# A two-layer mixture-of-experts trunk: expert overflow worked off pair by pair while the weights are in place

## The chip, the cores and the metric

The kernel runs on one NeuronCore of a Trainium2 chip, in one launch. The metric is device time in microseconds (us), the median of several executions. The engines are TensorE (PE, its weight loads shown as PEld), VectorE (DVE), ScalarE (ACT), GpSimd (POOL) and SyncE (SP, which issues nearly all weight transfers).

## What is computed

A trunk of two layers over 256 tokens of width 1024, in float32. Each layer mixes the tokens by four attention branches and then sends every token to 2 of 32 experts, each a gated feed-forward network of width 512:

```python
expert = (g_idx * EXPERTS_PER_GROUP + e_loc).reshape(-1)       # two experts for each token
...
def run_block(args):
    e, idx, g = args
    xb = xt[idx]
    hb = jax.nn.silu(xb @ w1[e]) * (xb @ w3[e])
    return (hb @ w2[e]) * g[:, None].astype(x.dtype)
...
y = jnp.zeros_like(xt).at[tok_buf].add(y_buf.reshape(-1, d))
```

The router chooses one of four groups and two of its eight experts, so an expert can get any number of tokens. With the reference's inputs the largest count is 27 in layer 0; in layer 1 one expert of 32, number 19, gets 33 tokens and no other more than 30. Only the numbers in the inputs decide that; the program is built without knowing them.

## The kernel before

**Pairs and places.** The 32 experts are taken two at a time: pair `i` (0 to 15) holds experts `2i` and `2i+1`. Each expert has `C = 32` places. A 0/1 matrix `Dm` (`placed`) puts tokens into places, `gather` (every fourth pair) collects the inputs of the next four pairs by matmul, `up_proj` multiplies by `w1` and `w3`, `glu` forms the gated hidden values, `down` multiplies by `w2`, and `combine` adds the results to the tokens' sums `acc`, which stay in PSUM for a whole layer.

**The weight ring.** A pair's weights are 8 MB of `up` and 4 MB of `w2`. They stream from HBM through `Ring`: 22 slots of 1 MB in the expert stage, made of eight tiles of two slots and six tiles of one. The list `jobs` gives the order of loads. `fill` goes through the list in order and stops at the first job that finds no room; a 2 MB job needs both slots of one tile, a 1 MB job takes a single slot first. `free` gives slots back and calls `fill`. This bookkeeping is done when the program is built; on the chip SP issues the loads in that order, and a load waits until the last reader of its slot is done. `up_parts` and `down_parts` say in how many jobs an expert's weights come. One further 1 MB tile (`early`) lies outside the ring and holds one part of pair 0.

**Order of the work.** PE's order is written out by hand (`manual_schedule`). The loop at L1437 lets the up-projection of pair `i` come before the down-projection of pair `i-1`; the loads are listed in that order too (`up(i)`, then `down(i-1)`). `up_proj` frees each part of the weights as soon as it has been used, `down` frees the rest. Pair 0's up-projection stands in `start_up` (L1190), ahead of the scatter matrix of pair 0 (L1193), which needs the gates `G` from `gates_of`.

**Overflow.** `overflow_list` counts how many further blocks of 32 places each expert needs and writes a list; it is advanced at pairs 4 to 6. At pair 7, `overflow` reads the count into every engine (L1213) and, if it is above zero, loops over the list (L1214): it loads that expert's weights once more by POOL's queue into ring slots held back for it (`over`, 5 MB from pair 5 to pair 7) and runs the block on its own.

Of the kernel before, what the change touches and what calls it, by code (L numbers as in the profile page):

```python
# [20 lines left out]
OVER = S * 2 // C  # L21
ALPHA = (2 * L) ** 0.25
# [24 lines left out]
def consts():  # L47
    p = np.arange(128)
    parts = {
        "ident": np.eye(128),  # L50
        "uinc": p[:, None] <= p[None, :],
        "ustr": p[:, None] < p[None, :],
        "causal": np.where(p[None, :] <= p[:, None], 0.0, NEG),
        "chunk": np.where(p[None, :] // 64 <= p[:, None] // 64, 0.0, NEG),
        "iota1": np.broadcast_to(np.arange(1, C + 1), (128, C)),
        "iota32": np.broadcast_to(np.arange(32), (128, 32)),
        "group": np.broadcast_to(np.arange(32) // 8, (128, 32)),
        "over": np.broadcast_to(C * np.arange(1, S // C), (128, S // C - 1)),
        "iota32c": p[:, None],
    }  # L60
# [54 lines left out]
def down_parts(e):  # L115

    return 2 if e < FINE - 2 else 1
# [84 lines left out]
def program(tc, I, out):  # L202
# [886 lines left out]
    def overflow_list(OH, pool, psp):  # L1089
# [8 lines left out]
        cnt = pool.tile([32, 2], F32, name="cnt")  # L1098
        V.tensor_copy(cnt[:, 0:1], T[:32, 0:1])
        V.tensor_scalar(act, K("over")[0:32], cnt[:, 0:1], None, op0=OP.is_lt)  # L1100
        V.tensor_reduce(cnt[:, 1:2], act, axis=AX.X, op=OP.add)
# [4 lines left out]
        lin = pool.tile([32, 2 * OVER + 1], F32, name="lin")  # L1106
# [9 lines left out]
        V.tensor_copy(lin[:, 2 * OVER:2 * OVER + 1], cnt[:, 1:2])  # L1116
        yield
        pl = psp.tile([128, 2 * OVER + 1], F32, name="T")
        nc.tensor.matmul(pl, ones[0:32], lin, start=True, stop=True)
        lst = pool.tile([128, 2 * OVER + 1], I32, name="lst")  # L1120
        V.tensor_copy(lst, pl)
# [5 lines left out]
    def experts(l, lg, logits, split, late, c2, acc, two_parts):  # L1127
# [4 lines left out]
        def start_up():  # L1132
# [51 lines left out]
            for tag, size in (("G", 64), ("neg", 2), ("ex", 32), ("gsm", 2), ("e2", 2), ("den", 1),  # L1184
                              ("hs", 512), ("Dg", 256)):
                p1.tile([128, size], F32, name="room", tag=tag)
# [24 lines left out]
        def overflow(lst, before):  # L1211

            n_over = nc.values_load(lst[0:1, 2 * OVER:2 * OVER + 1], min_val=0, max_val=OVER)  # L1213
            with tc.If(n_over > 0), tc.For_i(0, n_over, 1) as i:  # L1214
                ev = nc.values_load(lst[0:1, ds(i, 1)], engines=[mybir.EngineType.Pool, mybir.EngineType.DVE],
                                    min_val=0, max_val=NE - 1)
                W = [ring[(l, "over", j)] for j in range(2)]
                for j in range(2):
                    nc.gpsimd.dma_start(W[j], wup[l, ds(ev, 1)].rearrange("o p k s f -> (o p) (k s f)")[:, 4096 * j:4096 * j + 4096])
# [24 lines left out]
                for k in range(8):  # L1244
                    w = W[k // 4].rearrange("p (k s f) -> p k s f", k=4, s=2)
                    for s in range(2):
                        nc.tensor.matmul(ph[C * s:C * s + C], xo[:, k], w[:, k % 4, s], start=k == 0, stop=k == 7)
                nc.gpsimd.dma_start(W[0], wdown[l, ds(ev, 1)].rearrange("o p a j f -> (o p) (a j f)"))
# [10 lines left out]
                w = W[0].rearrange("p (a j d) -> p a j d", a=2, j=4)  # L1259
# [83 lines left out]
        def gated(i):  # L1343

            Dg = p1.tile([128, 2, 2, 2 * C], F32, name="Dg")
            c0 = 2 * C * (i % PQ)
            D4 = Dm[i // PQ].bitcast(F32)[:, :, c0:c0 + 2 * C].rearrange("p t (e s) -> p t e s", e=2)
            gv = G[:, :, 2 * i:2 * i + 2, None].to_broadcast([128, 2, 2, C])
            for a in range(2):
                nc.vector.tensor_tensor(Dg[:, :, a].rearrange("p t (e s) -> p t e s", e=2), D4, gv, op=OP.mult)  # L1350
            return Dg

        def scatter(i, Dg):

            pd = wkp.tile([128, 2, 128], F32, name="px" if i else "T")
# [6 lines left out]
            st[i] = dict(DT=DT, gate=gate)  # L1362

        def up_proj(i, bank="ph"):

            x = xg[i // PQ]
            c0 = 2 * C * (i % PQ)
            ph = wkp.tile([128, FE], F32, name=bank)
            part = 8 // up_parts(2 * i)
            for k in range(8):  # L1370
                keys = [(l, "up", 2 * i + e, k // part) for e in range(2)]
# [6 lines left out]
                if k % part == part - 1:  # L1378
# [9 lines left out]
        def glu(i, hs):  # L1388
# [10 lines left out]
            gTs[i] = gT  # L1399

        def down(i):
# [3 lines left out]
            keys = [[(l, "w2", 2 * i + e, a) for a in range(parts)] for e in range(2)]  # L1405
            py = wkp.tile([128, 512], F32, name="py")
            for j in range(4):
                for a in range(2):
                    for e in range(2):
                        w = ring[keys[e][a % parts]].rearrange("p (a j d) -> p a j d", a=2 // parts, j=4)  # L1410
                        o = C * (2 * a + e)
                        nc.tensor.matmul(py[o:o + C], gTs[i][:, j, e], w[:, 0 if parts == 2 else a, j],  # L1412
                                         start=j == 0, stop=j == 3)
            ring.free(*keys[0], *keys[1])
            gate = st[i]["gate"]
# [4 lines left out]
        def combine(i):  # L1420

            for t in range(2):
                for j in range(2):
                    for a in range(2):
                        r = slice(2 * C * a, 2 * C * a + 2 * C)
                        nc.tensor.matmul(acc[t][a], st[i]["DT"][r, t], out_parts[r, j], start=False,  # L1426
                                         stop=i == n - 1 and j == 1, skip_group_check=True)
                if i == n - 1:
# [7 lines left out]
        with tc.manual_schedule(engines={mybir.EngineType.PE}):  # L1436
            for i in range(n):  # L1437
                q, last = i // PQ + 1, i == n - 1
                if i:
                    hs = evacuated(up_proj(i))  # L1440
                    down(i - 1)
# [13 lines left out]
                if not last:  # L1455
                    scatter(i + 1, Dg)
                if i % PQ == PQ - 1 and not last:
                    for _ in gather(q):
                        pass
                if 4 <= i < 7:  # L1460
                    found = next(listing)
                if i == 7:
                    overflow(*found)
                    ring.free(*[(l, "over", j) for j in range(3)])
            down(n - 1)
            combine(n - 1)
# [34 lines left out]
def layout(inputs):  # L1501
# [18 lines left out]
    d["params"] = pack({"ident": C["ident"], "ln0": ln[0], **{n: C[n] for n in ("ustr", "iota1", "iota32", "group", "over", "iota32c")},  # L1520
# [34 lines left out]
```

## Time and profile before

| what | value |
|---|---|
| median of 3 runs | 1460.35 us (1459.32 to 1461.28) |
| the profiled execution | 1461.55 us, span 1459.9 us |
| mean granted TensorE clock | 0.899 of full speed |
| PE busy | 1162.8 us (80% of the span) |
| DVE, ACT, POOL busy | 524.3, 371.4, 89.0 us |
| moved by DMA | 494.89 MB, mean 339 GB/s |
| expert stage, layer 0 (first up-projection to last combine) | 276.37 to 705.60 us |
| expert stage, layer 1 | 978.21 to 1445.29 us |

The times are from one profiled execution; a group of instructions is written with its line, its engine, what it writes and reads, its count and its mean. In slices of the span a digit is a busy share in tenths. "Idle before" names what ended the wait.

### The profile page before, as it was taken

The numbers are of one execution on the slowest core, as the hardware profiler recorded it, in microseconds if no ns is written. First come the engines' busy times: TensorE is split into PE (matmuls) and PEld (weight loads), VectorE is DVE, ScalarE is ACT, GpSimd is POOL, SyncE is SP. The second block draws the span as 40 slices with busy tenths as digits, with TensorE's granted clock in tenths as the row PEclk, the third lists the DMA queues.
The fourth block names the chain that finished last, engine by engine and source line by source line (L and its number), as shares of the span: only waits on it lengthen the run. The fifth ranks groups of instructions, "written<-read, shape, count | busy, mean of one in ns | idle before, by whom it ended". The sixth has DMA issues, their size and how long they took to land.

```text
span 1459.9 us, 19103 instructions
## 1 busy us (share of the span) xinstructions
PE 1162.8 (80%) x7762; PEld 694.2 (48%) x7766; DVE 524.3 (36%) x1308; ACT 371.4 (25%) x792; POOL 89.0 (6%) x86
## 2 busy tenths in 40 slices
PE   8999999877776667766899999988766588667664
PEld 8999998523212112211699999962311152112111
DVE  6667786521011001100576777762101021001103
ACT  5556555311001000100365655531100010001000
POOL 2000030230000000000200003013000000000001
PEclk9999999999787988878999999999888779888986
DMA  9433677699999999999934339759999986999995
GB/s 385 177 116 130 245 312 291 275 425 428 429 427 426 427 428 426 428 428 418 410 120 174 123 145 383 287 218 426 426 427 427 427 331 251 426 428 429 425 424 229
DMA packets 47257, 494.89 MB, mean 339 GB/s; under 512 B 4928, under 2 KB 8512, under 8 KB 12864
## 3 DMA queue, kind: packets, MB, share of 16 engines
q1 hardware_dynamic: 46016, 486.23, 80.7%
q0 software_dynamic: 432, 6.29, 1.1%
q8 instruction: 62, 1.02, 0.3%
q10 hardware_dynamic: 720, 1.12, 0.2%
q14 instruction: 27, 0.22, 0.0%
HBM read 492.58 MB, written 1.05 MB: 338 GB/s over the span
## 4 chain that ended last, share of the span: by engine, by line
DMA 35%; PE 23%; DVE 4%; issue 4%; ACT 1%; SPq 1%; POOLq 0%; DVEq 0%; POOL 0%; ACTq 0%
DMA wslot<-in_up_dram 17%; DMA wslot<-in_down_dram 15%; PE ph L1376 5%; PE py L1412 4%; PE mm L503 3%; PE mm L505 3%; PE mm L504 2%; DMA wslot<-in_wmix_dram 1%; DMA ap<-in_attp_dram 1%; DVE split L474 1%; PE po L604 1%; SPq L259 1%; PE lg L505 1%; PE lg L503 1%; PE lg L504 1%
## 5 line engine op out<-in xcount | busy, mean ns | idle before, releaser
L1376 PE MATMUL ph<-wslot,xg 128*32 128x512 f32 x2048 | 315.8, 687 | 124.8 <-DMA wslot<-in_up_dram 119.5
L1412 PE MATMUL py<-wslot,gT 128*32 128x512 f32 x1024 | 190.6, 793 | 104.9 <-DMA wslot<-in_down_dram 104.8
L1418 DVE SCALAR_TENSOR_TENSOR ys<-py,gate,ys 128x512 fp32r<-128x512 f32 x32 | 24.0, 750 | 696.4 <-ACT ys L1417 696.4
L1376 PEld LDWEIGHTS ph<-wslot,xg 128*32 128x32 f32 x2048 | 76.4, 123 | 335.9 <-DMA wslot<-in_up_dram 174.0
L474 DVE TENSOR_TENSOR split<-wslot,split 128x512 fp32r<-128x512 f32 (+1 forms) x272 | 191.5, 716 | 96.2 <-ACT split L473 62.6
L473 ACT ACTIVATE split<-wslot 128x512 fp32r<-128x512 f32 (+2 forms) x276 | 168.8, 616 | 141.6 <-PE mm L505 121.8
L503 PE MATMUL mm<-hThi,split 128*128 128x256 f32 x704 | 202.5, 288 | 0.0
L505 PE MATMUL mm<-hThi,split 128*128 128x256 f32 x704 | 197.8, 281 | 0.5
L504 PE MATMUL mm<-hTlo,split 128*128 128x256 f32 x704 | 196.8, 279 | 0.0
L1412 PEld LDWEIGHTS py<-wslot,gT 128*32 128x32 f32 x1024 | 42.5, 138 | 243.6 <-DMA wslot<-in_down_dram 131.7
L1385 ACT ACTIVATE hs<-ph 128x512 f32<-128x512 f32 x32 | 19.1, 597 | 479.9 <-PE ph L1376 479.9
L503 PEld LDWEIGHTS mm<-hThi,split 128*128 128x128 f32 x704 | 132.5, 188 | 3.7 <-ACT split L473 1.3
L505 PEld LDWEIGHTS mm<-hThi,split 128*128 128x128 f32 x704 | 132.3, 188 | 2.6 <-DVE split L474 2.5
L504 PEld LDWEIGHTS mm<-hTlo,split 128*128 128x128 f32 x704 | 132.5, 188 | 0.5 <-issue 0.5
L1417 ACT ACTIVATE ys<-py,gate 128x512 fp32r<-128x512 f32 x32 | 22.0, 687 | 270.9 <-PE py L1412 270.9
L1426 PE MATMUL acc<-ys,DT 64*128 64x512 f32 x256 | 46.9, 443 | 19.5 <-ACT ys L1417 10.4
L1426 PEld LDWEIGHTS acc<-ys,DT 64*128 64x128 f32 x256 | 21.5, 184 | 39.9 <-ACT ys L1417 19.3
L574 ACT ACTIVATE P<-P,mx 128x128 f32<-128x128 f32 (+1 forms) x80 | 35.5, 445 | 14.2 <-DVE mx L572 14.2
L505 PE MATMUL lg<-oT,split 128*128 128x256 f32 x128 | 36.1, 282 | 1.4 <-DVE split L474 1.3
L503 PE MATMUL lg<-oT,split 128*128 128x256 f32 x128 | 36.0, 282 | 0.2
L504 PE MATMUL lg<-oT,split 128*128 128x256 f32 x128 | 35.8, 279 | 0.0
L828 ACT ACTIVATE gt<-mm,hbg 128x256 f32<-128x256 f32 x64 | 26.8, 470 | 25.0 <-PE mm L505 25.0
(341 smaller groups left out, 1422.9 us busy)
## 6 DMA issues: line engine op xcount, KB each, us to landing
wslot<-in_up_dram SPq DMA_DIRECT2D x96, 2048.0 KB, 27.6
wslot<-in_down_dram SPq DMA_DIRECT2D x52, 2048.0 KB, 28.9
wslot<-in_wmix_dram SPq DMA_DIRECT2D x32, 2048.0 KB, 8.7
wslot<-in_up_dram SPq DMA_DIRECT2D x64, 1024.0 KB, 10.7
wslot<-in_down_dram SPq DMA_DIRECT2D x24, 1024.0 KB, 15.3
wslot<-in_up_dram POOLq DMA_DIRECT2D x2, 2048.0 KB, 19.5
wslot<-in_wmix_dram SPq DMA_DIRECT2D x4, 832.0 KB, 13.6
wslot<-in_lnrows_dram SPq DMA_DIRECT2D x3, 1024.0 KB, 17.7
```

The source lines that it names most:

```text
L473: nc.scalar.activation(hi, w, AF.Copy)
L474: engine.tensor_tensor(lo, w, hi.bitcast(F32), op=OP.subtract)
L503: nc.tensor.matmul(ps, st[0], mv[0], start=start, stop=False)
L504: nc.tensor.matmul(ps, st[0], mv[1], start=False, stop=False)
L505: nc.tensor.matmul(ps, st[1], mv[0], start=False, stop=stop)
L574: nc.scalar.activation(dst, dst, AF.Exp, bias=mx[:, t, j:j + 1], scale=-1.0, accum_out=sm[:, t, j:j + 1])
L828: nc.scalar.activation(gt[:, j], pg[:, j], AF.Tanh, bias=hbg[:, cidx:cidx + 1], scale=0.5)
L1376: nc.tensor.matmul(ph[o:o + C], x[:, k, c0 + C * e:c0 + C * e + C], w[:, k % part, s], start=k == 0, stop=k == 7)
L1412: nc.tensor.matmul(py[o:o + C], gTs[i][:, j, e], w[:, 0 if parts == 2 else a, j], start=j == 0, stop=j == 3)
L1417: nc.scalar.activation(ys[:, 0], py, AF.Copy, scale=gate)
L1418: nc.vector.scalar_tensor_tensor(ys[:, 1], py, gate, ys[:, 0].bitcast(F32), op0=OP.mult, op1=OP.subtract)
L1426: nc.tensor.matmul(acc[t][a], st[i]["DT"][r, t], out_parts[r, j], start=False, stop=i == n - 1 and j == 1, skip_group_check=True)
```

## The change

- `overflow_list` now also gives, for each pair, the number of further blocks of its fuller expert. The old list keeps only the experts of the first and the last pair (`APART = (0, 15)`).
- The loop takes each pair to its end: up-projection, gated hidden values, down-projection, combine. Loads are listed in that order (`up(i)`, then `down(i)`), and `w2` comes as two 1 MB jobs for each expert except the last two.
- At the end of pairs 1 to 14 stands `again(i)`: every engine reads the pair's block count and branches; if it is above zero, a loop gathers the next 32 tokens of both experts and runs them with the weights that are in place. Only after it are the pair's 12 MB freed. Pairs 0 and 15 free their weights as they are used.
- The list is worked out within pair 0. One ring slot (`over`, 2) is held from pair 0 to the layer's end, 2 MB (`over`, 0) from pair 5 to pair 7; `overflow` for pairs 0 and 15 stays at pair 7 and reloads into that one tile.
- Pair 0's scatter matrix comes ahead of its up-projection.

The diff, cut to its core (left out: the constants, the arithmetic of the list, and arguments handed on):

```diff
 def down_parts(e):
-    return 2 if e < FINE - 2 else 1
+    return 1 if e >= NE - 2 else 2
...
-        for i in range(n + 1):
-            if i < n:
-                jobs += [job for both in zip(up(2 * i), up(2 * i + 1)) for job in both]
-            if i:
-                es = (2 * i - 2, 2 * i - 1)
-                jobs += down(es[0]) + down(es[1]) if i < n else last(es)
+        for i in range(n):
+            es = (2 * i, 2 * i + 1)
+            jobs += [job for both in zip(up(es[0]), up(es[1])) for job in both]
+            jobs += down(es[0]) + down(es[1]) if i < n - 1 else last(es)
+            if i == 0:
+                jobs += [((l, "over", 2), lambda t: None, 1)]
...
             if i == 5:
-                jobs += [((l, "over", 0), lambda t: None, 2), ((l, "over", 1), lambda t: None, 2),
-                         ((l, "over", 2), lambda t: None, 1)]
+                jobs += [((l, "over", 0), lambda t: None, 2)]
...
-            ph = up_proj(0)
             out_parts = flex.tile([128, 2, 512], F32R, name="ys", tag="A")
-            hs = evacuated(ph)
-            scatter(0, gated(0))
-            glu(0, hs)
             listing = overflow_list(OH, p1, wkp)
...
+        def again(i):
+            lst = found[0]
+            at = 2 * OVER + 1 + i
+            blocks = nc.values_load(lst[0:1, at:at + 1], min_val=0, max_val=S // C - 1)
+            with tc.If(blocks > 0), tc.For_i(0, blocks, 1) as b:
...
+                px = wkp.tile([128, 8, 2 * C], F32, name="py")
+                for k in range(8):
+                    for t in range(2):
+                        for i2, x in enumerate(two_parts):
+                            nc.tensor.matmul(px[:, k], x[:, t, k].bitcast(F32), Do[:, t], start=t == i2 == 0,
+                                             stop=t == i2 == 1)
+                affine_T(xo, px, 0)
+                DT, gate = scatter(gated(i, Do))
+                down(i, glu(evacuated(up_proj(i, xo, 0, False))), gate)
+                combine(DT, False)
...
-                if k % part == part - 1:
+                if free and k % part == part - 1:
                     ring.free(*keys)
...
-            ring.free(*keys[0], *keys[1])
...
+            found = None
+            DT, gate = scatter(gated(0, places(0)))
             for i in range(n):
-                q, last = i // PQ + 1, i == n - 1
-                if i:
-                    hs = evacuated(up_proj(i))
-                    down(i - 1)
+                q, last, apart = i // PQ + 1, i == n - 1, i in APART
+                hs = evacuated(up_proj(i, xg[i // PQ], 2 * C * (i % PQ), apart))
...
-                    Dg = gated(i + 1)
-                if i:
-                    glu(i, hs)
-                    combine(i - 1)
+                    coming = scatter(gated(i + 1, places(i + 1)))
+                if i == 0:
+                    next(listing)
+                if i % PQ == PQ - 1 and not last:
+                    for _ in gather(q):
+                        pass
+                gT = glu(hs)
+                if i == 0:
+                    next(listing)
...
+                down(i, gT, gate)
+                if apart:
+                    ring.free(*[key for keys in down_keys(i) for key in keys])
+                if i == 0:
                     found = next(listing)
+                combine(DT, last)
+                if not apart:
+                    again(i)
+                    ring.free(*[key for j in range(up_parts(2 * i)) for key in up_keys(i, j)])
+                    ring.free(*[key for keys in down_keys(i) for key in keys])
```

## Rows read from the trace of the kernel before

**Rows 1.** The page's slices of the span.

```profile
DMA  9433677699999999999934339759999986999995
```

**Rows 2.** Waits of PE, layer 0's expert stage: engine, line, releaser, total, times, longest.

```profile
PE ph L1376 <- DMA wslot<-in_up_dram: 57.6, 29, 3.9
PE py L1412 <- DMA wslot<-in_down_dram: 51.4, 16, 3.9
```

**Rows 3.** Windows: busy time of engines, granted clock, DMA share, GB/s.

```profile
400.00:500.00 100.00, 68.30 (x419) 21.76 (x416) 14.95 (x41) 7.92 (x15) 0.00 (x0) 0.86 1.01 427
269.00:270.00 1.00, 1.00 (x5) 1.00 (x6) 0.97 (x4) 0.00 (x0) 0.00 (x0) 0.50 0.11 41
278.00:279.00 1.00, 1.00 (x16) 0.29 (x12) 0.54 (x5) 0.39 (x3) 0.00 (x0) 1.00 0.00 0
280.00:281.00 1.00, 1.00 (x13) 0.26 (x8) 0.49 (x3) 0.65 (x4) 0.00 (x0) 1.00 0.92 377
```

**Rows 4.** Windows around the overflow of layer 1.

```profile
1190.00:1200.00 10.00, 10.00 (x43) 5.44 (x45) 2.16 (x9) 0.00 (x0) 0.48 (x1) 0.66 0.32 136
1200.00:1210.00 10.00, 5.53 (x21) 1.32 (x18) 0.57 (x2) 0.87 (x2) 0.04 (x1) 0.85 0.58 210
1210.00:1220.00 10.00, 9.63 (x22) 2.73 (x20) 1.36 (x2) 0.00 (x0) 0.00 (x0) 0.98 0.01 2
1220.00:1230.00 10.00, 9.91 (x80) 3.54 (x84) 0.00 (x0) 0.60 (x1) 0.00 (x0) 0.83 0.91 361
```

**Rows 5.** DMA queues: what POOL's own queue moved.

```profile
q0 software_dynamic: 432, 6.29, 1.1%
```

**Rows 6.** Timeline, start of layer 0's expert stage: start, duration, instruction.

```profile
276.37 7.07 PE L1376 MATMUL ph<-wslot,xg 128*32 128x512 f32 x64
278.32 0.80 SPq L282 DMA_DIRECT2D wslot<-in_up_dram  x2
282.34 0.49 DVE L1350 TENSOR_TENSOR Dg<-Dm,G 128x128 f32<-128x128 f32 x2
283.37 0.44 PE L1357 MATMUL T<-cp,Dg 128*128 128x128 f32 x2
```

**Rows 7.** Timeline, down-projections and a combine.

```profile
292.41 3.62 PE L1412 MATMUL py<-wslot,gT 128*32 128x512 f32 x32
...
297.67 0.95 PE L1426 MATMUL acc<-ys,DT 64*128 64x512 f32 x6 [0.28 <-DVE ys L1418]
...
336.37 5.33 PE L1412 MATMUL py<-wslot,gT 128*32 128x512 f32 x30 [3.80 <-DMA wslot<-in_down_dram]
```

**Rows 8.** The branch not taken in layer 0: its instructions, then the timeline.

```profile
L1213 PEldq TENSOR_LOAD <-lst x1: 492/492/492, 466.7 to 466.7; - x1
L1214 PEldq EVENT_SEMAPHORE  x1: 51/51/51, 467.9 to 467.9; - x1
467.58 0.28 PE L1316 MATMUL px<-Dm,lo 128*128 128x256 f32 x1
467.98 0.81 SPq L282 DMA_DIRECT2D wslot<-in_up_dram  x2
469.28 1.06 PE L1376 MATMUL ph<-wslot,xg 128*32 128x512 f32 x6 [1.42 <-ACTq L1214]
473.55 2.79 PE L1376 MATMUL ph<-wslot,xg 128*32 128x512 f32 x12 [3.21 <-issue]
```

**Rows 9.** The branch taken in layer 1: timeline.

```profile
1180.94 0.23 DVE L1222 TENSOR_SCALAR ope<-pos,before 128x2 f32 x1 [1.05 <-issue]
1193.87 0.61 PE L1240 MATMUL T<-cp,wslot 128*32 128x128 f32 x2
1207.57 5.00 PE L1264 MATMUL py<-wslot,wslot 128*32 128x512 f32 x8 [3.78 <-DMA wslot<-in_down_dram]
1220.09 8.77 PE L1376 MATMUL ph<-wslot,xg 128*32 128x512 f32 x64 [0.47 <-PE acc L1268]
1220.20 0.81 SPq L282 DMA_DIRECT2D wslot<-in_up_dram  x2
```

More of the change, by code (lines that the diff above doesn't have):

```diff
@@ L21 @@
 OVER = S * 2 // C
+APART = (0, NE // 2 - 1)
 ALPHA = (2 * L) ** 0.25
@@ L1097, in overflow_list @@
         act = pool.tile([32, nb], F32, name="act")
-        cnt = pool.tile([32, 2], F32, name="cnt")
+        cnt = pool.tile([32, 3], F32, name="cnt")
         V.tensor_copy(cnt[:, 0:1], T[:32, 0:1])
         V.tensor_scalar(act, K("over")[0:32], cnt[:, 0:1], None, op0=OP.is_lt)
-        V.tensor_reduce(cnt[:, 1:2], act, axis=AX.X, op=OP.add)
+        V.tensor_reduce(cnt[:, 2:3], act, axis=AX.X, op=OP.add)
+        V.tensor_scalar(act, act, K("apart")[0:32], None, op0=OP.mult)
+        V.tensor_scalar(cnt[:, 1:2], cnt[:, 2:3], K("apart")[0:32], None, op0=OP.mult)
         yield
@@ L1105, in overflow_list @@
         sel = pool.tile([32, 3, nb, OVER], F32, name="sel", tag="hs")
-        lin = pool.tile([32, 2 * OVER + 1], F32, name="lin")
+        n_l = 2 * OVER + 1
+        lin = pool.tile([32, n_l + 32], F32, name="lin", tag="ex")
         rk = pool.tile([32, nb], F32, name="rk")
@@ L1216, in overflow @@
                                     min_val=0, max_val=NE - 1)
-                W = [ring[(l, "over", j)] for j in range(2)]
-                for j in range(2):
-                    nc.gpsimd.dma_start(W[j], wup[l, ds(ev, 1)].rearrange("o p k s f -> (o p) (k s f)")[:, 4096 * j:4096 * j + 4096])
+                W = ring[(l, "over", 0)]
                 pe = p1.tile([128, 2], F32, name="ope")
@@ L1353, in scatter, with places @@
-        def scatter(i, Dg):
-            pd = wkp.tile([128, 2, 128], F32, name="px" if i else "T")
+                nc.vector.tensor_tensor(Dg[:, :, a].rearrange("p t (e s) -> p t e s", e=2),
+                                        D.rearrange("p t (e s) -> p t e s", e=2), gv, op=OP.mult)
+            return Dg
+        def places(i):
+            c0 = 2 * C * (i % PQ)
+            return Dm[i // PQ].bitcast(F32)[:, :, c0:c0 + 2 * C]
+        def again(i):
[3 more added lines that the diff above has]
+            with tc.If(blocks > 0), tc.For_i(0, blocks, 1) as b:
+                pe = p1.tile([128, 2, 2], F32, name="ope")
+                nc.vector.tensor_scalar(pe.rearrange("p t e -> p (t e)"), pos[:, :, 2 * i:2 * i + 2], K("over")[:, ds(b, 1)],
+                                        None, op0=OP.subtract)
+                Do = area(0, 2, 2 * C)
+                nc.vector.tensor_tensor(Do.rearrange("p t (e s) -> p t e s", e=2),
+                                        io[:, None, None, :].to_broadcast([128, 2, 2, C]),
+                                        pe[:, :, :, None].to_broadcast([128, 2, 2, C]), op=OP.is_equal)
+                xo = area(128, 8, 2 * C)
+                px = wkp.tile([128, 8, 2 * C], F32, name="py")
[8 more added lines that the diff above has]
+                combine(DT, False)
@@ L1356, in scatter @@
+        def scatter(Dg):
+            pd = wkp.tile([128, 2, 128], F32, name="px")
             for t in range(2):
@@ L1361, in scatter, with up_keys, down_keys, up_proj @@
             nc.vector.tensor_reduce(gate, pd.rearrange("p t s -> p (t s)"), axis=AX.X, op=OP.add)
[L1362 to L1368, printed above, removed]
+            return DT, gate
+        def up_keys(i, j):
+            return [(l, "up", 2 * i + e, j) for e in range(2)]
+        def down_keys(i):
+            return [[(l, "w2", 2 * i + e, a) for a in range(down_parts(2 * i))] for e in range(2)]
+        def up_proj(i, x, c0, free):
+            ph = wkp.tile([128, FE], F32, name="ph")
             part = 8 // up_parts(2 * i)
             for k in range(8):
-                keys = [(l, "up", 2 * i + e, k // part) for e in range(2)]
+                keys = up_keys(i, k // part)
                 for e in range(2):
@@ L1386, in evacuated, with glu @@
             return hs
-        def glu(i, hs):
+        def glu(hs):
             gT = p1.tile([128, 4, 2, C], F32, name="gT", bufs=2)
@@ L1398, in glu, with down @@
             nc.vector.scalar_tensor_tensor(gT.rearrange("p j e c -> p (j e) c"), th, 0.5, v[:, :, 1], op0=OP.mult, op1=OP.mult)
-            gTs[i] = gT
-        def down(i):
+            return gT
+        def down(i, gT, gate):
             parts = down_parts(2 * i)
-            keys = [[(l, "w2", 2 * i + e, a) for a in range(parts)] for e in range(2)]
+            keys = down_keys(i)
             py = wkp.tile([128, 512], F32, name="py")
@@ L1418, in down, with combine @@
             nc.vector.scalar_tensor_tensor(ys[:, 1], py, gate, ys[:, 0].bitcast(F32), op0=OP.mult, op1=OP.subtract)
-        def combine(i):
+        def combine(DT, last):
             for t in range(2):
@@ L1425, in combine @@
                         r = slice(2 * C * a, 2 * C * a + 2 * C)
-                        nc.tensor.matmul(acc[t][a], st[i]["DT"][r, t], out_parts[r, j], start=False,
-                                         stop=i == n - 1 and j == 1, skip_group_check=True)
-                if i == n - 1:
+                        nc.tensor.matmul(acc[t][a], DT[r, t], out_parts[r, j], start=False,
+                                         stop=last and j == 1, skip_group_check=True)
+                if last:
                     for a in range(2):
@@ L1454, in experts @@
                     next(residual)
[L1455 to L1460, printed above, removed]
-                    found = next(listing)
+                down(i, gT, gate)
+                if apart:
+                    ring.free(*[key for keys in down_keys(i) for key in keys])
+                if i == 0:
+                    found = next(listing)
+                combine(DT, last)
[3 more added lines that the diff above has]
+                    ring.free(*[key for keys in down_keys(i) for key in keys])
                 if i == 7:
                     overflow(*found)
-                    ring.free(*[(l, "over", j) for j in range(3)])
-            down(n - 1)
-            combine(n - 1)
+                    ring.free((l, "over", 0))
+                if not last:
+                    DT, gate = coming
+            ring.free((l, "over", 2))
             if l < L - 1:
```

33 lines of the change are left out of this document (18 added, 15 removed).

## The prediction

> **What bounds the kernel now.** I read the slices of the span first. The DMA engines are full, or nearly so, through both expert stages, except for one dip in layer 1 [rows 1]; before each stage they run out of work. PE's waits in layer 0's stage then name nothing but weights: 57.6 us for `up` and 51.4 us for `w2` [rows 2]. A window in the middle shows the same: 427 GB/s at a full DMA share, PE busy for 68 of 100 us [rows 3]. So the stage lasts as long as its transfers, plus any time in which no transfer runs. One ring slot (1.05 MB) takes 1.0486/427 = 2.46 us, a pair's twelve 29.5 us. A change counts here by the bytes that it saves and by the time in which the transfers stand still.
>
> They stand still twice. At the start of the stage the ring is full and nothing has been used: 41 GB/s at 269 us, none at 278, 377 again at 280 [rows 3], because the first slots come free only in the first up-projection, which begins at 276.37 [rows 6]. And in layer 1 the overflow stops SP in its loop: 136, 210, 2 and 361 GB/s in four windows of 10 us [rows 4]. Against 427 that lacks 2.9 + 2.2 + 4.3 + 0.7 = 10.0 MB, or 23.4 us. POOL's queue moved 6.29 MB more than a run without overflow needs [rows 5], or 14.7 us. Together the overflow costs 38.1 us. The two stages agree: by the times in the table above, that of layer 1 is 467.1 us long and that of layer 0 429.2, a difference of 37.9.
>
> **Part 1: the overflow's reload goes.** Expert 19 is in pair 9, which is worked off in place. The 38.1 us are gained, and what the new branch costs in pair 9 is set against them in part 4. Layer 0 has no overflow and gains nothing.
>
> **Part 2: the start.** Pair 0's scatter matrix now stands ahead of its up-projection in PE's hand-written order. Its input `Dg` is ready at 282.83 (282.34 + 0.49), and its transposes ran at 283.37 without waiting for PE's result [rows 6]. With them first, the up-projection begins at about 283.3 instead of 276.37, 6.9 us later, and nothing covers this, since the transfers already stand still. After such a wait PE is slow: an up-projection took 8.77 us after the overflow's half-clock stretch [rows 9] and 7.07 at full clock [rows 6]. I take 1.7 us more for the first freed slots. Start: 8.6 us in each layer (6.9 as the lower bound).
>
> **Part 3: slots come free later.** Today each part of `up` is freed as it is used. For pairs 1 to 14 all 12 slots now come free together, after combine and the branch. I followed the ring's own rule slot by slot (22 slots; a 2 MB job needs a whole tile) with durations from rows. From the landing of a pair's last weights: the down-projection takes 5.3 us (5.33 after a wait), ACT, DVE and combine another 2.6 (from 292.41 + 3.62 to 297.67 + 0.95) [rows 7].
>
> The branch: PE's register load starts at 466.7 and its closing semaphore at 467.9, while PE's last matmul ends at 467.86; SP issues at 467.98 [rows 8]. So the slots were released about 0.1 us after PE's work. Then PE ran six matmuls and stood 3.21 us with no releaser, having waited 1.42 before [rows 8]. Combine is a shorter cover than that gather, so I take 0.6 us for the release; the bounds are 0.1 and 4.6 (1.42 + 3.21, if the pause came first). The 4.6 us of PE are hidden wherever PE waits for weights afterwards. From SP's issue to flow is 1.4 us (278.32 to between 279 and 280.5) [rows 3, 6]. In sum 5.3 + 2.6 + 0.6 + 1.4 = 9.9 us pass before transfers for the next room flow.
>
> What covers these 9.9 us is what the ring can load ahead. By megabytes it would be 22 - 1 (held) - 12 = 9 slots, 22 us. But `w2` in 1 MB jobs breaks up two-slot tiles, and the list stops at the first job without room. The count gives four or six slots ahead in most pairs (9.8 or 14.7 us), so 9.9 us just fits, and only two (4.9 us) while `over` holds a tile. Pair by pair, the time without transfers:
>
> Pair 1: pair 0 frees 11 slots, 27.0 us of work. They run dry 3.5 (the first quarter of `up`, twice 1.77 at half clock) + 1.4 + 27.0 = 31.9 us after the first up-projection begins. Pair 0 then takes 8.8 (up) + 1.5 (evacuation and transposes) + 1.7 (`glu`) + 1.0 (the list, moved here; an estimate from its few short DVE steps) + 3.6 + 2.6 = 19.2, and pair 1 takes 7.1 + 1.5 + 1.7 + 3.6 + 2.6 + 0.6 = 17.1. With 1.4 to flow that is 37.7: 5.8 us lost. Pair 2 begins after the branch's pause and has eight slots' work ahead: 3.2. Pair 3, with a gather: 1.5. Pairs 5, 6 and 7, with `over` held: 5.0 + 3.3 + 2.1. The others: 0.6 together. In each layer 8.6 + 5.8 + 3.2 + 1.5 + 10.4 + 0.6 = 30.1 us.
>
> The same count with the order of before, the overflow left out, gives 703.2 us for the end of layer 0's stage, where the trace has 705.60.
>
> **Part 4: the branch taken.** Today's loop body runs from DVE's first step at 1180.94 to SP's next issue at 1220.20, 39.3 us, of which PE waited 3.8 for the reload [rows 9]; the way in adds some 1.5. That makes 37 us. The new body has both experts in it, but the up-projection's four column groups run side by side in either case, and combine is shorter. The bounds are 25 (today's PE work of about 33 us ran in good part at half clock, 0.66 granted in one window [rows 4]; at full clock some 12 go) and 49 (the gather, 12.3 us to 1193.87, doubles with its columns). No slot comes free meanwhile: 5.3 + 2.6 + 37 + 1.4 = 46.3 us against 9.8 of transfers ahead, a stop of 36.4 us. So the stop alone takes back nearly the whole gain, though no byte is loaded twice.
>
> **Edits at nothing.** The last pair's tail keeps its order, and the last weights arrive when they did. The list's extra steps are in pair 0. Register loads of ACT, DVE, POOL and SP run ahead of their next work. Behind each branch SP queues only loads that wait for that pair's slots anyway; without that cover they would cost what PE pays.
>
> **The sum.** On the profiled execution: 1461.55 - 38.1 + 2 x 30.1 + 36.4 = 1520. That execution lies 1.2 us above the median, so 1519.
>
> [...] The row shows PE going on for six matmuls behind a branch and pausing only then [rows 8]. [...]
>
> **The rivals.** *Every release waits for the code.* The new body is longer, so the target may lie farther off, and the 4.6 us may fall before PE's closing semaphore. Then 13.9 us pass instead of 9.9; pairs with four slots ahead no longer fit. The count gives 62.9 us for each layer and 30.6 for the taken branch: 1461.55 - 38.1 + 125.8 + 30.6 - 1.2 = 1579. For it: the pause exists. Against it: in the one row it came after.
>
> *The room counts by megabytes.* If nine slots are ahead after all (22.1 us), only the start and pair 1 cost (14.4 each layer), and the taken branch costs 46.3 - 22.1 = 24.2: 1475. Against it: the rule of the two-slot tiles.
>
> *The other side: only the start is paid.* If slots come free early enough that no later stop is left, the taken one included, 1461.55 - 38.1 + 17.2 - 1.2 = 1439. It is faster from the point where the stops of both layers sum to less than 38.1 us. For it: PE idles nearly a third of the stage. Against it: the room ahead is shorter than the loop body by any count.
>
> **How the numbers follow.** My count 0.50, with its own range 1500 to 1550 (release at 0.1 to 2 us, body at 25 to 49); every release late 0.28; room by megabytes 0.12; only the start 0.05; something between, near no change, 0.05. The range, 1488 to 1588, takes in the first two with the bounds. A difference of 0.2% is about what a measurement here can tell from none. Faster 0.06, same 0.03, slower 0.91; the time is that of my count, 1519.
>
> **What the new profile would show.** Right: the first `ph` matmuls in each layer some 7 us later behind PE's transposes; DMA windows below 427 GB/s at pairs 1, 2 and 5 to 7; one stop of 30 to 40 us in layer 1's middle; POOL's queue without its 6.29 MB. Every pair with a dip would mean the first rival; dips only at pair 1 and pair 9 the second. The forecast is wrong if the ring's room ahead is not what I counted, or if the release after the branch is far from 0.6 us.

## The result and the profile after

The changed kernel takes 1557.8 us (median of 4 runs, 1555.8 to 1559.3), against 1459.84 for the kernel before, run beside it: 1.067 times as long, interval 1.065 to 1.069. The forecast was 1519, with a range of 1488 to 1588. The profiled execution's span is 1556.4 us.

The slices of the page and one of its queues (the answers to [rows 1, 5]):

```profile
DMA  9333867689988989899934357659898889299996
...
q8 instruction: 103, 1.69, 0.4%
```

POOL's own queue, with its 6.29 MB [rows 5], is gone: the reload is away. But where nearly every slice of an expert stage had 9 tenths [rows 1], layer 0's stage now has five of 8, and layer 1's four of 8 and one of 2. The waits of PE show a new line (engine, line, releaser, total, times, longest):

```profile
PE ph L1412 <- DMA wslot<-in_up_dram: 165.9, 53, 9.9
PE ph L1412 <- PEq L1365: 61.0, 24, 6.5
...
PE px L1389 <- DVE Dg L1352: 13.1, 2, 6.5
```

L1365 is the `If` of the new branch: 24 times PE's next up-projection waited for PE's own sequencer. Windows of layer 0's middle and of the taken branch in layer 1 (columns as in [rows 3]):

```profile
400.00:500.00 100.00, 62.27 (x370) 20.62 (x368) 11.69 (x27) 7.16 (x13) 0.00 (x0) 0.83 0.94 390
...
1320.00:1330.00 10.00, 8.13 (x50) 2.36 (x46) 1.60 (x4) 0.98 (x2) 0.00 (x0) 0.78 0.99 419
1330.00:1340.00 10.00, 8.71 (x74) 6.26 (x66) 1.76 (x5) 0.69 (x1) 0.00 (x0) 1.00 0.27 112
1340.00:1350.00 10.00, 9.53 (x87) 4.20 (x85) 2.77 (x10) 0.16 (x1) 0.00 (x0) 1.00 0.00 0
1350.00:1360.00 10.00, 5.96 (x48) 2.21 (x52) 2.36 (x6) 1.51 (x3) 0.00 (x0) 1.00 0.01 2
```

390 GB/s stand where the kernel before has 427 [rows 3]. The taken branch stops the transfers for three windows, which lack 315 + 427 + 425 GB/s against 427, or 11.7 MB, or 27 us; some 2 us of these are what a pair loses anyway (below). PE runs the whole body at the granted clock 1.00.

The timeline of layer 0's start answers to [rows 6], and shows the scatter matrix first; the gather ahead of it ended some 3 us earlier than before, so that the up-projection begins 4.0 us later than in [rows 6], and some 7 us behind the gather instead of at once:

```profile
279.18 0.49 DVE L1352 TENSOR_TENSOR Dg<-Dm,G 128x128 f32<-128x128 f32 x2
...
279.82 0.66 PE L1389 MATMUL px<-cp,Dg 128*128 128x128 f32 x2 [6.55 <-DVE Dg L1352]
...
280.41 8.47 PE L1412 MATMUL ph<-wslot,xg 128*32 128x512 f32 x64
```

Two timelines at the ends of pairs 1 and 2 show the two kinds of release:

```profile
313.83 0.97 PE L1460 MATMUL acc<-ys,DT 64*128 64x512 f32 x6 [0.29 <-DVE ys L1452]
314.94 2.85 SPq L293 DMA_DIRECT2D wslot<-in_down_dram  x3
...
315.12 1.45 PE L1412 MATMUL ph<-wslot,xg 128*32 128x512 f32 x9 [0.32 <-PEq L1365]
...
331.70 0.96 PE L1460 MATMUL acc<-ys,DT 64*128 64x512 f32 x6 [0.29 <-DVEq L1365]
...
338.30 0.81 SPq L284 DMA_DIRECT2D wslot<-in_up_dram  x2
...
338.48 1.92 PE L1412 MATMUL ph<-wslot,xg 128*32 128x512 f32 x6 [5.82 <-PEq L1365]
```

After pair 1, SP issues 0.14 us behind combine (313.83 + 0.97 to 314.94). After pair 2 it issues 5.64 us behind it, and PE goes on only then. The line's own answer gives the branch instruction on PE, first in all, then in a window on each of these two (count, then least, median and longest duration in ns):

```profile
L1365 PEldq COMPARE_BRANCH  x31: 80/629/6616, 314.4 to 1512.3; - x31
...
L1365 PEldq COMPARE_BRANCH  x1: 371/371/371, 314.4 to 314.4; - x1
...
L1365 PEldq COMPARE_BRANCH  x1: 6032/6032/6032, 332.1 to 332.1; - x1
```

14 of the 28 pairs with a branch show one of 1.9 to 6.6 us, 67 us in sum; the others stay under 0.8. So both the forecast's count (release 0.6 us behind combine) and its first rival (every release late) describe about half of the pairs. For each pair I also worked out the transfers' loss: from one combine's end to the next, less the megabytes moved in between (the window's GB/s) at 427 GB/s. Before it is about 0 in nearly every pair; now it is 0.5 to 5.4 us in each of layer 0, 42 in sum.

### The profile page after: what moved, and what is told of

It is laid out like the page before. It is cut to its first block, busy times and chain, and to the rows that moved or that the text cites. A ratio compares the mean times of both kernels' runs of the same rounds, so it can differ in the third digit from the quotient of the medians.

```text
span 1556.4 us, 19679 instructions
## 1 busy us (share of the span) xinstructions
PE 1160.7 (75%) x7814; PEld 692.9 (45%) x7814; DVE 541.1 (35%) x1316; ACT 374.8 (24%) x793; POOL 87.5 (6%) x83
## 5 line engine op out<-in xcount | busy, mean ns | idle before, releaser
L1412 PE MATMUL ph<-wslot,xg 128*32 128x512 f32 x2048 | 356.7, 777 | 242.9 <-DMA wslot<-in_up_dram 165.9
L1412 PEld LDWEIGHTS ph<-wslot,xg 128*32 128x32 f32 x2048 | 83.9, 136 | 498.4 <-issue 275.1
L1448 PE MATMUL py<-wslot,gT 128*32 128x512 f32 x1056 | 149.8, 642 | 51.2 <-issue 29.8
L1392 DVE TENSOR_SCALAR DT<-px 128x256 fp32r<-128x256 f32 x33 | 14.0, 424 | 493.5 <-PE px L1389 493.5
L1352 DVE TENSOR_TENSOR Dg<-Dm,G 128x128 f32<-128x128 f32 x64 | 24.0, 413 | 84.6 <-PEq L1365 83.1
L506 PE MATMUL lg<-oT,split 128*128 128x256 f32 x128 | 36.1, 282 | 1.4 <-DVE split L475 1.3
L504 PE MATMUL lg<-oT,split 128*128 128x256 f32 x128 | 36.0, 281 | 0.2
```

The costliest lines, as they stand in the source:

```text
L504: nc.tensor.matmul(ps, st[0], mv[0], start=start, stop=False)
L506: nc.tensor.matmul(ps, st[1], mv[0], start=False, stop=stop)
L1412: nc.tensor.matmul(ph[o:o + C], x[:, k, c0 + C * e:c0 + C * e + C], w[:, k % part, s], start=k == 0, stop=k == 7)
L1448: nc.tensor.matmul(py[o:o + C], gT[:, j, e], w[:, 0 if parts == 2 else a, j], start=j == 0, stop=j == 3)
```

## The experiments

The theory from this profile was that freeing together and the pause in the branch both cost, with the start on top. The first four kernels ran on one chip. The interval is that of the ratio to the kernel before, which had 1460.94 us.

**The branch left out.**

```
-                    again(i)
```

> The changed kernel without its branch: the register load, the If and the loop behind combine are left out; slots of the 14 pairs still come free together behind combine. Leaves out the tokens past the 32 places in pairs 1 to 14 (here one token of expert 19 in layer 1). Theory (late release, part of it paid in the branch): PE's 24 long pauses in the branch go (61 us in sum, about half of it not covered by weights on their way), and the stop of about 24 us in pair 9 goes: 1557.8 - 24 - 2 x 16 = about 1502, and every pair's first slot comes free within 0.2 us of combine's end. Rival 1 (the pauses in the branch cost nothing because PE would wait for weights anyway): only the taken branch goes, 1557.8 - 24 = about 1534. Rival 2 (the branch is everything, freeing together costs nothing): about 1422 + 17 = 1440.

Measured: 1446.6 us (0.991, 0.989 to 0.992), 111 us less than the changed kernel; the theory had said 56. Not one pair loses more than 0.5 us of transfers apart from the last. The window 400 to 500 us of this kernel:

```profile
400.00:500.00 100.00, 66.20 (x395) 21.40 (x393) 11.40 (x28) 7.76 (x14) 0.00 (x0) 0.86 1.01 424
```

My reading of the edit was wrong in one point: SP doesn't issue behind combine here, but runs ahead. A load waits for the last instruction that read its slot. With the body gone this is the up-projection, whatever line frees the slot. So this run took away the late release too, and more had to be told apart.

**The branch with a body of one memset.**

```
-            with tc.If(blocks > 0), tc.For_i(0, blocks, 1) as b:
...
+            with tc.If(blocks > 0):
+                nc.vector.memset(area(0, 2, 2 * C), 0.0)
```

> The changed kernel with the branch in every pair, but its body is one small memset of VectorE instead of the whole second pass; nothing else of the pair's end moves. Leaves out what no_branch leaves out. Theory (the pause is code that has to be fetched because the target lies a long body behind the branch): PE's body is empty, the long pauses of 2 to 6.6 us vanish, the time is that of no_branch plus 14 x 2 x at most 0.5, between 1502 and 1510. Rival 1 (the register load and the compare cost it, or it's where other traffic delays any fetch): pauses stay in about half of the pairs and the time is that of no_branch plus about 32, some 1534. Rival 2: the branch costs nothing in either kernel, and both stand near 1534.

Measured: 1447.7 us (0.991, 0.989 to 0.993). A branch in 28 pairs costs about 1 us in all when its body is short and reads no slot. The branch instruction on PE:

```profile
L1365 PEldq COMPARE_BRANCH  x29: 70/202/325, 317.9 to 1404.4; - x29
```

**More room: `up` in 1 MB jobs.**

```
-    return 4 if e < FINE or e >= NE - 2 else 2
+    return 4
```

> The changed kernel with the up weights of all experts loaded in quarters of 1 MB (one slot each) instead of halves of 2 MB (a whole two-slot tile each); the branch and the frees stay. Theory (the stops come from the count of room: a 2 MB job waits for a whole tile, and what stands behind it in the list waits too): about nine slots ahead instead of four to six, so most stops of 2 to 5 us vanish; the count gives 27 and 32 us less for the two layers, about 1499. Rival 1 (the stops are the pauses of PE's branch themselves, whatever room there is): within 10 us of 1557.8. Rival 2 (smaller transfers run slower or cost SP more, as would show in full windows below 427 GB/s): slower than 1557.8.

Measured: 1501.5 us (1.027, 1.026 to 1.029), 56 us less; the count had said 59. The branch still pauses 6 us in half of the pairs, but with more slots ahead the transfers lose only 0.4 to 0.7 us in pairs 3 to 14 of layer 0. Its branch and its window:

```profile
L1365 PEldq COMPARE_BRANCH  x31: 70/447/6207, 314.3 to 1456.2; - x31
...
400.00:500.00 100.00, 63.19 (x378) 19.85 (x382) 11.88 (x28) 7.16 (x13) 0.00 (x0) 0.84 1.01 419
```

**The start undone.**

```
-            DT, gate = scatter(gated(0, places(0)))
             for i in range(n):
...
+                if i == 0:
+                    DT, gate = scatter(gated(0, places(0)))
```

> The changed kernel with pair 0's up-projection put back ahead of pair 0's scatter matrix in PE's order. Theory (the start is paid in full, nothing covers it): the first up-projection begins 6.5 us earlier in each layer and at full clock, so 2 x (6.9 + 1.7) = 17 us less, about 1541. Rival (pair 0 frees so much at once that a later stop, at pair 1 or 2, takes up what the start gains): between 1553 and 1558.

Measured: 1553.0 us (1.063, 1.058 to 1.068; four runs spread over 1543.8 to 1559.5): 5 us less and not 17; with this spread the 5 can hardly be told from none. The windows of this kernel and of the changed one say where the rest went. Up_first:

```profile
300.00:308.00 8.00, 6.21 (x54) 1.91 (x46) 1.60 (x4) 0.98 (x2) 0.00 (x0) 0.93 0.84 346
308.00:315.00 7.00, 5.58 (x40) 1.70 (x36) 1.41 (x3) 0.69 (x1) 0.56 (x1) 0.84 0.00 0
```

The changed kernel:

```profile
300.00:308.00 8.00, 6.81 (x62) 2.18 (x54) 1.08 (x3) 0.98 (x2) 0.00 (x0) 1.00 1.02 420
308.00:315.00 7.00, 5.11 (x40) 1.61 (x40) 1.31 (x4) 0.69 (x1) 0.00 (x0) 1.00 0.69 288
```

The first up-projection begins 5.6 us earlier (all but two of its matmuls, at 274.78 against 280.41), but pair 1's slots come free behind its branch at 314.3 instead of 314.9. What pair 0 freed earlier is used up earlier, and the transfers stand still until pair 1's end.

The next four, against 1459.72 us, tell the late release from the pause.

**Late release without a branch.**

```
-                    again(i)
+                    touch(i)
...
+            for n_key, key in enumerate(keys):
+                o = C * (n_key % 4)
+                nc.tensor.matmul(ph[o:o + C], ident[:, 0:C], ring[key][:, 0:512], start=True, stop=True)
```

> no_branch, with 12 short matmuls on PE behind combine that read one 512-column piece of each of the pair's 12 slots, so that the slots' last reader stands at the pair's end, as in the changed kernel, without any branch. Leaves out the second pass of pair 9. In no_branch the last reader of an up slot is the up-projection itself, so there the slots came free as used, whatever line frees them; that run took away the late release and the branch together, 111 us. Theory (both cost: late release by the count, and the pause on top): the count with a release 0.1 to 1.0 us behind combine gives 18 to 25 us more than no_branch for each layer, 1447 + 36 to 50 = 1483 to 1497. Rival 1 (late release costs nothing, all is the pause): 1447 to 1453. Rival 2 (all is late release, the pause is hidden): 1557.8 - 24 = about 1530.

Measured: 1514.2 us (1.038, 1.036 to 1.040), 68 more than no_branch and more than the theory's 36 to 50. SP issues 1.01 us behind combine here in nearly every pair. The 50 already took in a release that late, so the count of what late release costs is too low by some 18. In the next kernel the 12 matmuls stand in a body that is skipped and push no release back.

**Late release with a short branch.**

```
-            with tc.If(blocks > 0), tc.For_i(0, blocks, 1) as b:
...
+            with tc.If(blocks > 0):
+                nc.vector.memset(area(0, 2, 2 * C), 0.0)
+                touch(i)
```

> The changed kernel with the body of its branch cut to one memset and the same 12 short matmuls on the pair's slots, in every pair; never taken in pairs other than 9. Leaves out the second pass of pair 9. Theory (the pause comes from the length of the body): no PE pause above 0.5 us in the branch, SP's next load 0.1 to 0.3 us behind combine in every pair, and the time of held_no_branch plus at most 10. Rival (the branch itself, whatever its body, makes the wait): pauses of 2 to 6 us remain and the time is 40 us or more above held_no_branch.

Measured: 1499.4 us (1.027, 1.025 to 1.029). The branch never takes more than 0.33 us on PE, SP issues 0.13 us behind combine in nearly every pair, and yet the time is 52 us above the memset body. The only difference is that the body, hardly ever executed, has 12 matmuls that read the slots. For a release at 0.1 us the count had given 36.

```profile
L1365 PEldq COMPARE_BRANCH  x29: 70/207/332, 316.1 to 1460.1; - x29
...
400.00:500.00 100.00, 63.33 (x356) 19.45 (x356) 10.95 (x26) 7.15 (x13) 0.00 (x0) 0.80 0.92 384
```

In layer 0 the transfers lose 5.2 and 4.8 us in pairs 6 and 7, where `over` holds a tile, 1.3 to 3.3 in the other pairs up to 13, and 33 in sum. Pair 12 shows what the count had too small:

```profile
650.67 5.32 PE L1440 MATMUL py<-wslot,gT 128*32 128x512 f32 x26 [0.68 <-DMA wslot<-in_down_dram]
...
658.63 0.81 SPq L284 DMA_DIRECT2D wslot<-in_up_dram  x2
...
658.00:659.00 1.00, 0.69 (x8) 0.24 (x6) 0.00 (x0) 0.00 (x0) 0.00 (x0) 1.00 0.24 98
659.00:660.00 1.00, 0.86 (x4) 0.00 (x0) 0.00 (x0) 0.00 (x0) 0.00 (x0) 1.00 1.01 229
660.00:661.00 1.00, 0.56 (x8) 0.26 (x12) 0.00 (x0) 0.00 (x0) 0.00 (x0) 1.00 0.44 164
```

SP issues 8.0 us after the last weights let the down-projection go on, as counted (5.3 + 2.6 + 0.1), and four slots, 9.8 us of transfers, were still to come. But the rate has fallen before SP issues and is full again only 2.4 us after it. The three windows lack 0.8 MB, 1.9 us, where the count, with full rate to the last byte and 1.4 us from issue to flow, had next to nothing.

**The long body, but without the slots.**

```
+                other = two_parts[0][:, 0].bitcast(F32).rearrange("p k q -> p (k q)")[:, 0:512]
...
-                down(i, glu(evacuated(up_proj(i, xo, 0, False))), gate)
+                down(i, glu(evacuated(up_proj(i, xo, 0, False, other))), gate, other)
...
+                                         w[:, k % part, s] if other is None else other,
...
```

> The changed kernel with the whole body, instruction for instruction, but its matmuls on weights read a piece of the activations instead of the ring's slots, so that the body doesn't hold them. Its second pass works on wrong weights. Theory (the pause matters only because the release waits for it): PE's pauses of 2 to 6.6 us in the branch stay in about half of the pairs, yet transfers run at 425 GB/s through the pairs, and the time is 1447 plus 0 to 15 for the branch taken in pair 9. Rival (the pause costs PE time that the stage needs): 1447 + 40 to 60 = about 1500.

Measured: 1482.0 us (1.016, 1.014 to 1.017). The pauses are all there (14 of 5.9 to 6.8 us), and the transfers run on:

```profile
L1365 PEldq COMPARE_BRANCH  x31: 70/702/6772, 315.5 to 1435.5; - x31
...
L1365 SPq EVENT_SEMAPHORE  x11: 27/28/20797, 1235.9 to 1285.0; - x11
...
400.00:500.00 100.00, 64.49 (x386) 21.19 (x382) 11.40 (x26) 7.15 (x13) 0.00 (x0) 0.84 1.01 423
```

In pair 9 they lose 23.6 us, nearly as much as in the changed kernel, though this body holds no slot: SP itself waits in the loop, 20.8 us on one semaphore. The rest, 1482.0 - 23.6 - 1447.7 = 11 us, is left for the pauses when no release waits for them. My bound of 1462 was too low: I had allowed at most 15 us for the taken branch.

**The second pass ahead of the main one.** The whole computation is done.

```
+                if not apart:
+                    again(i)
-                hs = evacuated(up_proj(i, xg[i // PQ], 2 * C * (i % PQ), apart))
+                hs = evacuated(up_proj(i, xg[i // PQ], 2 * C * (i % PQ), True))
...
-                if not apart:
-                    again(i)
-                    ring.free(*[key for j in range(up_parts(2 * i)) for key in up_keys(i, j)])
-                    ring.free(*[key for keys in down_keys(i) for key in keys])
```

> The changed kernel with the branch of pairs 1 to 14 put ahead of the pair's own up-projection instead of behind its combine; the slots are freed as the main pass uses them, and the two scatter matrices are two fixed tiles. The whole computation is done. Theory (the branch costs when it is the last reader of the slots): the main pass is the last reader again; the pauses stay but lie where PE waits for weights, and the body of pair 9 runs while that pair's weights and the next ones still land, so 1447 plus 0 to 10, faster than before. Rival 1 (the pauses shift every up-projection and so every release): about 1447 + 40 to 60 = 1500. Rival 2 (the taken branch stops the transfers by its 24 us here too): about 1471.

Measured: 1481.0 us (1.016, 1.014 to 1.017): 77 us less than the changed kernel, yet not the theory's 1447 to 1457. The taken branch now costs the transfers only 7 us. But pairs 1 and 2 of layer 0 lose 2.3 and 8.9 us, and pair 2 of layer 1 loses 6.4. There, I take it, the ring is still full from its start, so PE is what the transfers wait for, and a pause of 6 us ahead of an up-projection delays its frees. The next kernel tries that. Of the 33 us above small_body these losses make 25; the others are not placed.

**That, without a branch in pairs 0 to 2, and the start undone.**

```
-APART = (0, NE // 2 - 1)
+APART = (0, 1, 2, NE // 2 - 1)
...
```

The rest of the edit is that of again_ahead and that of up_first.

> again_ahead, and pair 0's up-projection again ahead of its scatter matrix, and pairs 1 and 2 listed with 0 and 15 for the loop that reloads, so that no branch stands in the pairs in which the ring still works off its full start. The whole computation is done. In again_ahead the transfers still lost 2.3 and 8.9 us in pairs 1 and 2 of layer 0, 6.4 in pair 2 of layer 1, and some 12 us at each start. Theory (these losses go, the taken branch keeps its 7): 1481 - 17 - 2 x 7 to 9 = 1446 to 1450, faster than the kernel before. Rival (the start's gain is taken up by a later stop, as in up_first): 1460 to 1464, no change against before.

Measured: 1449.8 us (0.9925, 0.991 to 0.994, five runs, against 1460.55): 0.7% faster than the kernel before, and within the theory's range. With the reference's inputs no expert of pairs 0 to 2 overflows; where one does, it is loaded again. The windows around the taken branch of this kernel:

```profile
1220.00:1230.00 10.00, 9.59 (x84) 8.12 (x88) 2.61 (x11) 0.00 (x0) 0.00 (x0) 1.00 1.01 428
1230.00:1240.00 10.00, 6.16 (x44) 1.50 (x40) 1.18 (x5) 0.00 (x0) 0.00 (x0) 0.88 1.01 425
1240.00:1250.00 10.00, 7.05 (x54) 1.90 (x46) 0.94 (x3) 1.67 (x3) 0.00 (x0) 0.95 0.82 350
1250.00:1260.00 10.00, 8.40 (x73) 2.98 (x73) 1.14 (x3) 0.00 (x0) 0.00 (x0) 1.00 0.67 238
```

The body runs while weights land, and what is left of the stop of 27 us is 77 + 189 GB/s in two windows, 6 us.

**The old overflow's price, and the start's without a late release.** The first leaves out `overflow(*found)` in the kernel before, the second makes the edit of up_first in no_branch.

> The kernel before without the call of its overflow loop: no register load, no If, no reload. Leaves out the tokens past the 32 places. Theory (the prediction's part 1: reload 14.7 us and stop 23.4 us in layer 1): 1461.55 - 38.1 - 1.2 = about 1422. Rival (only the megabytes count, the stop is made up by the ring's room): about 1445.

> no_branch with pair 0's up-projection put back ahead of its scatter matrix. Leaves out the second pass of pair 9. In up_first, with the branch, this edit gave 5 us instead of 17, and the transfers stood still 6.9 us at pair 1 instead: there pair 1's slots came free only behind its branch. Theory (without a late release nothing takes the gain up): 1446.6 - 2 x (6.9 + 1.7) = about 1429. Rival (the start is worth only what up_first showed): 1440 to 1444.

Measured: 1422.45 us (0.973, 0.972 to 0.975), as forecast, so the old overflow costs 1460.55 - 1422.45 = 38.1 us; and 1431.6 us (0.980, 0.978 to 0.982), so the start costs 1446.6 - 1431.6 = 15.0, near the 17.2 that were forecast.

**`w2` in whole jobs.**

```
-    return 1 if e >= NE - 2 else 2
+    return 2 if e < FINE - 2 else 1
```

> The changed kernel with the w2 weights of most experts loaded in one job of 2 MB again instead of two of 1 MB; the branch, the frees and the bytes stay. Theory (room is counted by the ring's rule, tile by tile: with 2 MB jobs alone only whole tiles serve, and odd single slots stay empty): the count puts 90 us of standing transfers into a layer where it puts 34 for the changed kernel, so 1557.8 + 2 x 56 = about 1670. Rival 1 (megabytes decide): within 10 us of 1557.8. Rival 2 (larger jobs fit better and help): under 1540.

Measured: 1683.5 us (1.152, 1.150 to 1.154, against 1461.06), 126 us more than the changed kernel where the count had said 112. Its branch and its window:

```profile
L1365 PEldq COMPARE_BRANCH  x31: 80/446/4267, 316.5 to 1651.0; - x31
...
400.00:500.00 100.00, 56.70 (x290) 15.85 (x282) 9.21 (x22) 5.01 (x9) 0.00 (x0) 0.72 0.85 356
```

The same bytes in larger jobs make it much slower; by the count, because they find no whole tile.

## Why the prediction was right in part, step by step

The medians give a ladder, from the kernel before to the changed one:

- Part 1, the old overflow: -38.1 us, forecast and measured.
- Part 2, the start: +15.0, forecast 17.2. Behind the late release it is worth some 5 at most (up_first), because pair 1's end then decides; the forecast added both in full.
- The remaining edits (no_branch_up_first less before_no_overflow): +9.1, forecast 0. The traces place about half of it: with one slot held from pair 0, a slot less has landed when each stage begins (below, up to 270 us, the first the kernel before without its overflow; layer 1 has the same difference), which is 2.46 us in each layer. The rest is spread over the stages (426 GB/s in the middle of layer 0's against 427) and not settled.

```profile
q1 hardware_dynamic: 8672, 64.40, 61.4%
q1 hardware_dynamic: 8528, 63.36, 60.3%
```

- A branch with a short body (small_body less no_branch): +1.1, forecast 0.
- Part 3, slots freed together (short_slots less small_body): +51.7, forecast 43.0 (30.1 less the start's 8.6, twice) with a release at 0.6 us, and 36 by the same count at the 0.1 us that short_slots has. The mechanism is shown: the count of tiles foretold -59 and +112 for two other job sizes, and -56 and +126 came. In layer 0 of short_slots pairs 1, 2, 3 and 5 to 7 lose 19.2 us together, where the count gave 20.9. The term was undersized in the "others": 0.6 us together by the count, 14 measured (33.2 less 19.2); pair 12 above is one of them. By the same two runs the second rival, room by megabytes (1475), is out: the bytes stayed the same and the time moved by 182 us between them.
- The rest (the changed kernel less short_slots): +58.4. Of these about 25 are the taken branch. The other 33 are left for the pauses ahead of the release; added up pair by pair, the two traces' losses outside pair 9 differ by 28.

-38.1 + 15.0 + 9.1 + 1.1 + 51.7 + 58.4 = 97.2, against 97.96 between the two kernels' medians.

Two steps failed, in opposite directions. **"so I take 0.6 us for the release"** rested on the one branch of before, whose pause came six matmuls behind the branch [rows 8]. In the changed kernel the pause lies inside the branch instruction, ahead of the semaphore that releases the slots, in half of the pairs: SP issues 1.5 to 6.3 us behind combine instead of 0.6, beyond even the upper bound of 4.6. The first rival had put this into every pair, and its 1579 lies 21 us above, where 1519 lies 39 below. **"That makes 37 us"** for the taken body was too long: PE's part runs from 1334.9 to 1358.8, a little under the lower bound of 25. The half-clock stretches of the old loop (0.50 granted from 1184 to 1196 us and from 1208 to 1210; [rows 4, 9]) weren't part of the work: the new body's windows stand at 1.00. So the taken branch costs 25 us and not 36.4, which hid 11 us of the other error. Its reason, "No slot comes free meanwhile", is not all of it either: in long_no_slots the body holds none, and the stop is nearly as long, because SP waits in the loop. The result lies outside the count's own range, 1500 to 1550. The recorded range holds it because it took in the first rival too; that the time came no farther from 1519 is luck, since the two errors have opposite signs.

That the body's length makes the pause is shown by small_body, short_slots and long_no_slots: same place, same register load, 0.2 us with a short body and up to 6.8 with the long one (the short ones also lack the loop `For_i`, which no run varied alone). That PE waits for code in it I read from the DMA packets. The instruction queue q8 carries 103 packets of 16 KB instead of the 62 of small_body:

```profile
q8 instruction: 62, 1.02, 0.3%
```

13 of the 14 long pauses have a whole packet of it inside, and the shortest, of 1.9 us, the end of one; of the 17 short branch instructions one has. All 14 end 1.3 to 1.5 us after their packet. Why only half of the branches pay is not settled.

The rival "only the start is paid" (1439) needed the slots to come free early enough. That is what ahead_apart3 builds, but with the start undone too, for which that rival's sum would be 17.2 lower, 1422. It gives 1449.8: of the 27 us between them 6 are the taken branch and 9 the remaining edits, and 12 are not settled; long_no_slots left 11 for the pauses.

## What to carry to other kernels

A body that is almost never executed still counted here as a reader of what it reads: the buffers that it touches were held until the branch was passed, in every iteration (short_slots, 51.7 us above small_body). Put the rare pass ahead of the common one, so that the common one is the last reader, and where work is still waiting for data. That alone wasn't enough here (1481.0); the branch also had to leave the pairs in which nothing covers it. A skipped long body also made PE pause, 1.9 to 6.6 us in 14 of 28 pairs of the changed kernel, where a short one took at most 0.33, so let no release stand behind it. And a change of the order in which buffers come free has to be counted with the allocator's own units, here whole tiles, not in megabytes.

## What was not expected of the hardware

The pause has two lengths. In the changed kernel, layer 0's first long one is 6.03 us, with the transfers at full rate at its beginning; the one at the end of pair 7 is 3.27, with the transfers standing still. Windows in each, that of pair 7 first:

```profile
500.00:503.00 3.00, 0.00 (x0) 0.00 (x0) 0.14 (x1) 0.00 (x0) 0.00 (x0) 0.79 0.02 5
332.00:335.00 3.00, 0.66 (x6) 0.19 (x2) 0.00 (x0) 0.67 (x1) 2.20 (x2) 0.91 1.01 431
```

In up_small_jobs, whose transfers hardly ever stop, all 14 take 6.0 to 6.2 us; in w2_whole, with the emptiest queues, 3.3 to 4.3. The packets of q8 show where the difference lies: in the changed kernel the packet begins 0.9 to 1.4 us into the five long pauses in which the transfers stand still, and 3.3 to 4.2 us into the seven in which they run for most of the time; in w2_whole 0.9 to 1.7, in up_small_jobs 3.5 to 3.7. So here the packet of code came later while weights were on their way; that it waits behind them is not shown, since no run varied the load on the queues alone. And up_small_jobs, with all its expert weights but the last pair's `w2` in 1 MB jobs, fills its window at 419 GB/s, where small_body and no_branch, with `up` mostly in 2 MB jobs, have 424 to 425 (for 64 experts of 6.29 MB some 12 us of its 1501).
